# Gather buffers reused as weight buffers, earlier splits of the first tail weights, wider level spacing, one softmax step

## Chip, cores and metric

The kernel runs on one core of a Trainium2 chip. The metric is the device time of one execution in microseconds (us), lower is better. Before the change, three executions took 1249.47, 1243.44 and 1245.83 us, a median of 1245.83 us.

## What is computed

Two blocks in sequence on 256 tokens of width 1024, all float32. The first block ends in PEER: every token picks, in each of 8 heads, 16 of 16384 small experts, and sums their outputs. The second block sends its normalised input through four branches and merges them under gates.

```
act = gelu(einsum('td,thkd->thk', xb, u[expert]))             # 8 heads x 16 experts a token
h   = h + einsum('thk,thkd->td', g * act, v[expert])          # PEER, after a gated-linear-attention mixer
x   = rms_norm(h, norm_f_g)
cols = rms_norm(x, norm_pre) @ w_in_2                          # second block
y_a = deltanet(...); y_b = spatial_gating(gelu(gm_uv), ...)    # gm_uv: the columns called Z_GU, Z_GV here
y_c = sliding_window(softmax with one sink a head); y_m = memory_attention(...)
merged = sum over 4 branches of sigmoid(gate) * (y @ w_up);  out = x + rms_norm(merged @ w_out, norm_post)
```

## The kernel before

**Tiling.** Tokens go in two batches of 128 (b = 0, 1), one token a partition. Weights come as tiles of 128x1024 float32 (512 KB), four to a group, in one fixed order (`STREAM`). Groups named in `SPLIT` are multiplied in two parts: ScalarE (ACT) rounds a tile to `hi` (L207, `cut`), VectorE (DVE) or GpSimd (POOL) subtracts to get `lo` (L208), and TensorE (PE) makes three matmuls of 512 columns (L356 to L358) where a plain float32 product would take one.

**Front and gather stage.** After the first mixer (until about 144 us) the PEER runs in 256 slots, one per batch, head and rank (`peer`). A slot gathers 128 rows of 2048 float32 (1 MB) from `peer_uv` by an indirect DMA that POOL issues (L826) into a buffer `uv`; DVE takes the dot product with the first half of each row (L854); ACT does gelu, weight and diagonal (L858, L859, L865); PE adds the second half into `acc` (L877), or, in some slots, DVE adds it to `x` (L871). A buffer is free after that. Buffers come from `pair`: six of `pairs` at first, then, once the pool `early` of the second batch's mixer is closed (`more_pairs`), four more of `late`. The same pool `pairs` holds split weights (`wp`) in the front and in the tail.

**Order.** All instructions are in an order written out by hand through generators. `gathers` (L892) runs one slot of `peer` after another, and between slots a step of `routes` (expert selection) by a rate per slot and a step of `shadow`: the second batch's mixer, then memory projections, and, for the first batch of the second block, pre-norm, projections, delta net, `sliding(0)` and `memory_attn(0)`. `mixer_levels(1, 3)` takes one level per 3 + 1 steps. In `sliding`, the exponentials (L1355, L1358) are spread over five steps, so that gelus of slots stand between them; ACT loads a function table at each change between them (ACT_TABLE_LOAD).

**End of the gather stage.** `Z_GU`'s four tiles, loaded long before, are split after the last gather's issue (`n <= i < n + 4`, alternately DVE and POOL); `Z_GV`'s four tiles are loaded on ACT's DMA queue in four late sums. `last_out(1)` (L912) adds `acc`, takes two norms and the transposes that feed the second block, with `Z_GV`'s splits between its steps.

**Tail.** The second block's second batch and everything split runs from about 891 us. `wt` keeps `depth` = 4 further tiles loaded and `ahead` = 3 further tiles split, in program order of PE's use; tiles lie in the pool `big` of 28 buffers, in turn with other data. `SyncE` (SP) issues their loads, and a load waits until its buffer's last reader is done. Splits alternate between POOL (even tile) and DVE (odd tile). `pace` mixes branch work between the projections.

```
pair: k = turn["at"] % turn["ring"];  (pairs if k < N_PAIR else late["pairs"]).tile([P, 2048], ...)
AHEAD, LAG = (3, 4), (2, 3)     # slots from gather to dot, from dot to sum; with 6 and with 10 buffers
```

Of the kernel before, what the change touches and what calls it, by code (L numbers as in the profile page):

```python
# [9 lines left out]
F32 = mybir.dt.float32  # L10
# [4 lines left out]
AF = mybir.ActivationFunctionType  # L15
# [4 lines left out]
P = 128  # L20
T = 256
NB = T // P
# [5 lines left out]
N_SLOT, N_PAIR = 28, 6  # L28
# [107 lines left out]
def chain(*gens):  # L136
    for g in gens:
        yield from g
# [3 lines left out]
def kernel(ctx, tc, I, out, dbg=None):  # L142
# [6 lines left out]
    pairs = ctx.enter_context(tc.tile_pool(name="pairs", bufs=N_PAIR))  # L149
    work = ctx.enter_context(tc.tile_pool(name="work", bufs=2))  # L150
    psum = ctx.enter_context(tc.tile_pool(name="psum", bufs=3, space=PSUM))
    first, late = ctx.enter_context(ExitStack()), {}
    early = first.enter_context(tc.tile_pool(name="early", bufs=N_EARLY))
    ctx.enter_context(tc.manual_schedule())

    def slot(name, dt=F32):

        return big.tile([P, 1024], dt, tag="slot", name=name)
# [17 lines left out]
    def more_pairs():  # L176

        first.close()
        late["pairs"] = ctx.enter_context(tc.tile_pool(name="late", bufs=N_LATE))
        turn.update(at=N_PAIR, ring=N_PAIR + N_LATE)  # L180

    def dump(name, ap, view):
        if name in dbg:
# [15 lines left out]
    def load_to(n, queue=nc.sync):  # L199
        while state["next"] < min(n, 4 * G_END):  # L200
            i = state["next"]
            raw[i] = slot(f"w{i}")
            queue.dma_start(out=raw[i], in_=I["wts"][4 * STREAM[i // 4] + i % 4])
            state["next"] += 1

# [4 lines left out]
    def cut_to(n, eng=None):  # L210
        for i in range(state["cut"], min(n, state["next"])):
            if is_split(i):
                if i // 4 in (Z_GV, G_O2 + 1):
                    hi, lo = slot(f"wh{i}", F32R), slot(f"wl{i}", F32R)
                else:
                    wp = pair(f"wp{i}", F32R)
                    hi, lo = wp[:, :1024], wp[:, 1024:]
                cut(raw[i], hi, lo, eng or (G if state["pool"] and i % state["share"] == 0 else V))
                parts[i] = chunks(hi), chunks(lo)
        state["cut"] = max(state["cut"], min(n, state["next"]))  # L220
# [94 lines left out]
    def halves_rstd(x, junk, adds, meanwhile=lambda: None):  # L315

        ss = small("ssh", 2)
        for nh in range(2):
            s = slice(nh * 512, (nh + 1) * 512)
            adds[nh](s)  # L320
            S.activation(junk[:, s], x[:, s], AF.Square, scale=D ** -0.5, accum_out=ss[:, nh:nh + 1])
        r = rstd2(ss)
        meanwhile()
        return r
# [514 lines left out]
    def peer():  # L839


        n = len(all_slots)
        tiles, wv, dg, dve = {}, {}, {}, {}
        dots = diags = sums = 0
        for i in range(n + AHEAD[1] + LAG[1]):
            ahead, lag = AHEAD[state["late"]], LAG[state["late"]]
            state["left"] = n + ahead + lag - i
            if i < n:
                yield from until(routed, all_slots[i][:2])
                tiles[i] = gather(*all_slots[i])  # L850
            while dots < min(n, i - ahead + 1):
                b, h, s = all_slots[dots]
                t = tiles[dots][:, :D]
                V.scalar_tensor_tensor(t, t, 1.0, hn[b], op0=OP.mult, op1=OP.mult,  # L854
                                       accum_out=act[:, h, s:s + 1])
                yield from until(routed, (b, h, "w"))
                ge, wv[dots] = small("ge", 1), small("wv", 1, bufs=6)
                S.activation(ge, act[:, h, s:s + 1], AF.Gelu)  # L858
                S.activation(wv[dots], ge, AF.Copy, scale=gw[b][:, h, s:s + 1])  # L859
                dots += 1  # L860
            while diags < min(dots, i - ahead - lag + 3):
                dve[diags] = on_dve(*all_slots[diags])
                if not dve[diags]:
                    dg[diags] = small("dg", P, bufs=3)
                    S.activation(dg[diags], ident, AF.Copy, scale=wv[diags])  # L865
                diags += 1
            while sums < min(diags, i - ahead - lag + 1):
                b, h, s = x = all_slots[sums]
                t = tiles.pop(sums)[:, D:]
                if dve[sums]:  # L870
                    V.scalar_tensor_tensor(xr[b], t, wv[sums], xr[b], op0=OP.mult, op1=OP.add)  # L871
                else:
                    start = b not in acc
                    if start:
                        acc[b] = psum.tile([P, 2, 512], F32, tag="acc", bufs=1, name=f"acc{b}")
                    for nh in range(2):
                        TE.matmul(acc[b][:, nh], dg[sums], t[:, nh * 512:(nh + 1) * 512],  # L877
                                  start=start, stop=h == 7 and s == 15)
                    pe(1.8)
                if b == NB - 1 and h == 7 and 8 <= s < 12:  # L880
                    load_to(4 * Z_GU + 2 * (s - 7), S)
                if b and h == 0 and s == 1:
                    run(peer_out(b - 1))
                    routed["out", b - 1] = True
                sums += 1
            if n <= i < n + 4:
                cut_to(4 * Z_GU + 1 + i - n, G if i % 2 else V)
            yield

    def gathers(main, routes, rate, others):  # L890
# [25 lines left out]
    def last_out(b):  # L916

        x, junk, a, nf = xr[b], hn[b], acc[b], rowt["nf"]

        def add(s):  # L920
            V.tensor_tensor(out=x[:, s], in0=x[:, s], in1=a.rearrange("p a n -> p (a n)")[:, s], op=OP.add)

        def scale(s):
            V.scalar_tensor_tensor(x[:, s], x[:, s], r, nf[:, s], op0=OP.mult, op1=OP.mult)

        r = halves_rstd(x, junk, (add, add))
        cut_to(4 * Z_GV + 1, G)
        yield
        r2 = halves_rstd(x, junk, (scale, scale), lambda: cut_to(4 * Z_GV + 2, V))
        dump("x2", x, lambda d: d[b * P:(b + 1) * P])  # L930
        dr = small("dg", P, bufs=3)
        V.tensor_scalar(dr, ident, r2, None, op0=OP.mult)
        cut_to(4 * Z_GV + 4, G)
        yield
        hT[b] = slot3(f"hT{b}", 8)
        hh2[b] = slot3(f"hh{b}", 8, P, F32R), slot3(f"hl{b}", 8, P, F32R)

        def put(h, pt):
            s = slice(4 * h, 4 * h + 4)
            gained(hT[b][:, s], pt, chan[:, C_NP:C_NP + 8], h)  # L940
            cut(hT[b][:, s], *[t[:, s] for t in hh2[b]])

        yield from transposed(x, put, scale=dr)
# [386 lines left out]
    def sliding(b):  # L1330
# [21 lines left out]
        V.scalar_tensor_tensor(m, m, sc_, sk, op0=OP.mult, op1=OP.max)  # L1352
        V.tensor_scalar(nm, m, -1.0, None, op0=OP.mult)
        V.tensor_tensor(out=es, in0=sk, in1=m, op=OP.subtract)
        S.activation(es, es, AF.Exp)  # L1355
        yield
        for h in range(8):
            S.activation(sc[:, h], sc[:, h], AF.Exp, scale=sc_, bias=nm[:, h:h + 1], accum_out=su[:, h:h + 1])  # L1358
            if h % 2:
                yield  # L1360
        V.tensor_tensor(out=su, in0=su, in1=es, op=OP.add)
        V.reciprocal(su, su)
# [201 lines left out]

    def shadow():
        yield from rest
        yield from mixer_levels(1, 3)
        yield from mixer_out(1)
        score["mixed"] = True
        yield from peer_norm(1)  # L1570
        for h in range(8):
            yield from until(score, (0, "of", h))
            yield from peer_scores(1, h)
            if h == 4:
                load_memory()
                yield from step(block2_consts)
            if h == 6:
                load_to(4 * G_MEM + 4)
        state["depth"] = 4
        yield from memory()  # L1580
        yield from step(mask_swT)
        yield from until(routed, ("out", 0))
        yield 8.0
        yield from pre2(0)
        yield from small_proj(0)
        yield from qkv(0)
        yield from q_proj(G_SWQ, "swq", 0)
        yield from q_proj(G_XMQ, "xmq", 0)
        state["depth"] = 0
        yield from deltanet(0)  # L1590
        yield from together(sliding(0), memory_attn(0))
        pre2_cut(0)

    state["late"] = 0
    run(gathers(peer(), routes(), lambda i: 0.75 if i < 12 else 0.6 if i < 100 else 0.36, shadow()))
    state["pool"] = True


    rowt["gm"] = slot("row_gm")[:, :512]
    state["share"] = SHARE  # L1600

    state["ahead"] = -1
    lo, sp = last_out(1), chain(spatial_u(Z_GU, "gmu", [0]), spatial_u(Z_GV, "gmv", [0]))
    next(lo)
    for _ in range(4):
        next(sp)
    next(lo)
    for _ in range(2):
        next(sp)
    run(lo, sp)  # L1610
    state.update(depth=4, ahead=3)
    run(spatial_u(Z_GU, "gmu", [1]))
    run(spatial_u(Z_GV, "gmv", [1]))

    def tail_main():
        yield from small_proj(1)
# [116 lines left out]
```

## Time and profile before

| quantity | us |
|---|---|
| median of three executions | 1245.83 |
| the profiled execution, and its span | 1244.99, 1243.2 |
| PE busy | 1065.9 (86%) |
| DVE busy | 873.8 (70%) |
| ACT busy | 514.0 (41%) |
| POOL busy | 457.9 (37%) |
| L877 acc matmuls, 832 | 425.7 |
| L854 dots, 256 | 307.9 |

The page shows the DMA engines' mean share in 40 slices: 9 tenths or more from the 7th slice to the 27th (186 to 839 us), 7 in the 28th (839 to 870 us), and 6 to 0 afterwards. So the stages have different limits, and the rows below are taken by stage. A DMA share slightly over 1 is rounding of overlapping packets. A wait is idle time just before an instruction, with the event that came last.

### The profile page before, as it was taken

Reading aid. Unit: us, or ns where it says so; the run is one execution under the profiler, and the core shown is the slowest. Engines: PE = TensorE matmul, PEld = TensorE weight load, DVE = VectorE, ACT = ScalarE, POOL = GpSimd, SP = SyncE. Lnnn points to the kernel's source line nnn. Section 1 sums busy time; section 2 is a strip of 40 time slices with the busy share of each in tenths; the row PEclk is TensorE's granted clock in tenths of the full one; section 3 lists DMA queues with packets and bytes.
Section 4 is the critical chain, followed back from the end, with each engine's and each line's share of the span. In section 5 each row is a group of like instructions: output and inputs, shape, how many; then the busy total and the mean of one; then the engine's idle time right before and its main releaser. Section 6 shows DMA issues by size and latency. Waiting matters only on the chain.

```text
span 1243.2 us, 14731 instructions
## 1 busy us (share of the span) xinstructions
PE 1065.9 (86%) x4934; PEld 735.1 (59%) x4934; DVE 873.8 (70%) x1823; ACT 514.0 (41%) x1272; POOL 457.9 (37%) x331
## 2 busy tenths in 40 slices
PE   7999879879997969838878888878699899799987
PEld 6876535444565626315445445434389788687876
DVE  5598578896777688788889899754716476248554
ACT  5615233443443434324436444466533433244432
POOL 3314224343534344433433535633310333135531
PEclk9998979989999989969899989998889899899999
DMA  9626489999999999999999999997446433355620
GB/s 367 214 80 216 177 351 356 352 400 426 425 425 425 422 425 426 425 427 384 412 425 424 381 385 422 426 426 299 167 161 237 137 119 119 97 207 183 246 81 34
DMA packets 68074, 376.38 MB, mean 303 GB/s; under 512 B 7696, under 2 KB 8992, under 8 KB 35232
## 3 DMA queue, kind: packets, MB, share of 16 engines
q0 software_dynamic: 36864, 268.45, 52.5%
q1 hardware_dynamic: 28688, 101.47, 22.7%
q10 hardware_dynamic: 2448, 5.54, 1.2%
q8 instruction: 39, 0.64, 0.2%
q14 instruction: 35, 0.29, 0.1%
HBM read 374.38 MB, written 1.05 MB: 302 GB/s over the span
## 4 chain that ended last, share of the span: by engine, by line
PE 33%; DVE 29%; DMA 15%; issue 11%; ACT 7%; POOL 5%; ACTq 0%; POOLq 0%; DVEq 0%; SPq 0%
DMA uv<-in_peer_uv_dram,idx 11%; DVE uv L854 9%; PE acc L877 7%; DVE wp L208 3%; POOL wp L208 2%; DMA w<-in_wts_dram 2%; POOL uv L826 2%; DVE x L871 2%; PE qkv L382 2%; PE pq L382 1%; ACT wp L207 1%; PE mk L382 1%; PE gate L356 1%; PE gate L357 1%; PE gate L358 1%
## 5 line engine op out<-in xcount | busy, mean ns | idle before, releaser
L877 PE MATMUL acc<-uv,dg 128*128 128x512 f32 x832 | 425.7, 648 | 99.6 <-ACT dg L865 88.7
L826 POOL DMA_INDIRECT uv<-in_peer_uv_dram,idx x256 | 304.6, 1190 | 436.4 <-PE acc L877 278.1
L854 DVE SCALAR_TENSOR_TENSOR uv<-uv,hn 128x1024 f32<-128x1024 f32 x256 | 307.9, 1219 | 71.1 <-DMA uv<-in_peer_uv_dram,idx 66.0
L877 PEld LDWEIGHTS acc<-uv,dg 128*128 128x128 f32 x832 | 158.8, 205 | 284.7 <-issue 150.8
L208 POOL TENSOR_TENSOR wp<-w,wp 128x1024 fp32r<-128x1024 f32 x48 | 127.8, 2668 | 276.2 <-ACT wp L207 270.9
L858 ACT ACTIVATE ge<-act 128x1 f32<-128x1 f32 x256 | 51.6, 202 | 351.0 <-DVE uv L854 350.0
L208 DVE TENSOR_TENSOR wp<-w,wp 128x1024 fp32r<-128x1024 f32 x60 | 98.3, 1650 | 94.4 <-ACT wp L207 94.4
L207 ACT CAST wp<-w 128x1024 fp32r<-128x1024 f32 x108 | 108.1, 1047 | 51.5 <-DMA w<-in_wts_dram 36.8
L865 ACT ACTIVATE dg<-mats,wv 128x128 f32<-128x128 f32 x208 | 81.0, 390 | 24.6 <-PE acc L877 23.4
L859 ACT ACTIVATE wv<-ge,gw 128x1 f32<-128x1 f32 x256 | 75.4, 295 | 8.3
L382 PEld LDWEIGHTS pq<-hnT,w 128*128 128x128 f32 x512 | 61.5, 193 | 11.5 <-issue 11.0
L871 DVE SCALAR_TENSOR_TENSOR x<-uv,wv,x 128x1024 f32<-128x1024 f32 x48 | 61.5, 1282 | 4.9 <-ACT wv L859 4.9
L382 PE MATMUL pq<-hnT,w 128*128 128x128 f32 x512 | 62.3, 276 | 0.0
L357 PE MATMUL gate<-wp,hh 128*128 128x512 f32 x128 | 50.1, 392 | 1.9 <-DVE wp L208 1.9
L356 PE MATMUL gate<-wp,hh 128*128 128x512 f32 x128 | 51.7, 404 | 0.0
L358 PE MATMUL gate<-wp,hl 128*128 128x512 f32 x128 | 49.9, 390 | 0.0
L382 PEld LDWEIGHTS qkv<-hT,w 128*128 128x128 f32 x384 | 45.6, 195 | 4.9 <-issue 4.6
L382 PE MATMUL qkv<-hT,w 128*128 128x128 f32 x384 | 45.7, 278 | 0.0
L858 ACT ACT_TABLE_LOAD x24 | 30.8, 1283 | 10.6 <-DMA wsm<-in_w_small_dram 10.2
L1440 ACT ACTIVATE gate<-gate 128x512 f32<-128x512 f32 x16 | 9.6, 598 | 51.9 <-PE gate L358 49.3
L357 PEld LDWEIGHTS gate<-wp,hh 128*128 128x128 f32 x128 | 24.2, 189 | 6.9 <-DVE wp L208 2.4
L358 PEld LDWEIGHTS gate<-wp,hl 128*128 128x128 f32 x128 | 24.2, 189 | 5.2
(500 smaller groups left out, 1832.8 us busy)
## 6 DMA issues: line engine op xcount, KB each, us to landing
w<-in_wts_dram SPq DMA_DIRECT2D x184, 512.0 KB
uv<-in_peer_uv_dram,idx POOLq DMA_INDIRECT x256
w<-in_wts_dram ACTq DMA_DIRECT2D x4, 512.0 KB
wsm<-in_w_small_dram ACTq DMA_DIRECT2D x8, 132.0 KB
x<-in_x_dram SPq DMA_DIRECT2D x2, 512.0 KB
skT<-in_skT_dram ACTq DMA_DIRECT2D x2, 512.0 KB
mem<-in_mem_dram SPq DMA_DIRECT2D x2, 512.0 KB
out_dram<-o SPq DMA_DIRECT2D x4, 256.0 KB
```

Source lines behind the costliest of these rows:

```text
L207: S.copy(hi, x)
L208: (eng or V).tensor_tensor(out=lo, in0=x, in1=hi.bitcast(F32), op=OP.subtract)
L357: TE.matmul(ps, fh, sl, start=False, stop=False)
L358: TE.matmul(ps, fl, sh, start=False, stop=stop)
L382: TE.matmul(ps, wt(g, c)[:, s], x, start=c == 0, stop=c == KC - 1)
L826: G.indirect_dma_start(out=t, out_offset=None, in_=I["peer_uv"], in_offset=bass.IndirectOffsetOnAxis(ap=idx[b][:, h, s:s + 1], axis=0))
L854: V.scalar_tensor_tensor(t, t, 1.0, hn[b], op0=OP.mult, op1=OP.mult, accum_out=act[:, h, s:s + 1])
L858: S.activation(ge, act[:, h, s:s + 1], AF.Gelu)
L859: S.activation(wv[dots], ge, AF.Copy, scale=gw[b][:, h, s:s + 1])
L865: S.activation(dg[diags], ident, AF.Copy, scale=wv[diags])
L871: V.scalar_tensor_tensor(xr[b], t, wv[sums], xr[b], op0=OP.mult, op1=OP.add)
L877: TE.matmul(acc[b][:, nh], dg[sums], t[:, nh * 512:(nh + 1) * 512], start=start, stop=h == 7 and s == 15)
```

## The change

- `more_weights` closes the late gather buffers after the gathers and opens in their memory a pool `tail` of eight 128x1024 buffers for the tail's weights. The ring of `pair` goes back from ten to six. `depth` becomes 7, `ahead` 2 (they were 4 and 3). Six tiles of the next group(s) are asked for at once.
- `Z_GU`'s splits go from the drain into slots n-10, n-8, n-6 and n-4, all on DVE, into buffers of `big` (`Z_GV`'s now go into `pair`). Two of `Z_GV`'s tiles are loaded in these slots, on SP's queue; the other two after `more_weights`. `last_out` no longer has splits between its steps.
- In the tail's start, `Z_GU` of batch 1 comes before `Z_GV` of both batches.
- `mixer_levels(1, 4)`: one more step per level. `routes` goes at 0.58 instead of 0.6 steps per slot up to slot 100.
- `sliding(0)`'s exponentials are one step; `sliding(1)`, in the tail, keeps its steps.

```diff
+    def more_weights():
+        second.close()
+        late["weights"] = ctx.enter_context(tc.tile_pool(name="tail", bufs=2 * N_LATE))
+        turn.update(at=0, ring=N_PAIR)
...
-            raw[i] = slot(f"w{i}")
+            if "weights" in late:
+                raw[i] = late["weights"].tile([P, 1024], F32, tag="tail", name=f"w{i}")
+            else:
+                raw[i] = slot(f"w{i}")
...
-                if i // 4 in (Z_GV, G_O2 + 1):
+                if i // 4 in (Z_GU, G_O2 + 1):
...
-                if b == NB - 1 and h == 7 and 8 <= s < 12:
-                    load_to(4 * Z_GU + 2 * (s - 7), S)
...
-            if n <= i < n + 4:
-                cut_to(4 * Z_GU + 1 + i - n, G if i % 2 else V)
+            if n - 10 <= i < n - 2 and i % 2 == 0:
+                cut_to(4 * Z_GU + 1 + (i - n + 10) // 2, V)
+                load_to(4 * Z_GV + (i - n + 8) // 2)
...
         r = halves_rstd(x, junk, (add, add))
-        cut_to(4 * Z_GV + 1, G)
         yield
-        r2 = halves_rstd(x, junk, (scale, scale), lambda: cut_to(4 * Z_GV + 2, V))
+        r2 = halves_rstd(x, junk, (scale, scale))
...
-        cut_to(4 * Z_GV + 4, G)
...
-        S.activation(es, es, AF.Exp)
-        yield
+        if state["pool"]:
+            S.activation(es, es, AF.Exp)
+        yield
+        if not state["pool"]:
+            S.activation(es, es, AF.Exp)
         for h in range(8):
             S.activation(sc[:, h], sc[:, h], AF.Exp, ...)
-            if h % 2:
+            if h % 2 and state["pool"] or h == 7:
                 yield
...
-        yield from mixer_levels(1, 3)
+        yield from mixer_levels(1, 4)
...
-    run(gathers(peer(), routes(), lambda i: 0.75 if i < 12 else 0.6 if i < 100 else 0.36, shadow()))
+    run(gathers(peer(), routes(), lambda i: 0.75 if i < 12 else 0.58 if i < 100 else 0.36, shadow()))
...
+    more_weights()
     state["ahead"] = -1
-    lo, sp = last_out(1), chain(spatial_u(Z_GU, "gmu", [0]), spatial_u(Z_GV, "gmv", [0]))
+    lo, sp = last_out(1), spatial_u(Z_GU, "gmu", [0])
     next(lo)
...
-    run(lo, sp)
-    state.update(depth=4, ahead=3)
+    run(sp)
+    load_to(4 * Z_GV + 4)
+    run(lo)
+    state.update(depth=2 * N_LATE - 1, ahead=2)
+    load_to(4 * G_AGAIN + 2 * N_LATE - 2)
     run(spatial_u(Z_GU, "gmu", [1]))
-    run(spatial_u(Z_GV, "gmv", [1]))
+    run(spatial_u(Z_GV, "gmv"))
```

**Three places where instructions move.** On ACT, in the first batch's sliding attention (`sws` its scores, `sw_es` the sink, `ge`, `wv`, `dg` of the slots, `msc` the memory attention's scores), before:

```order
L1355 ACT_TABLE_LOAD
L1355 ACTIVATE sw_es<-sw_es 128x8
L858 ACT_TABLE_LOAD
L858 ACTIVATE ge<-act 128x1
L859 ACTIVATE wv<-ge,gw_137 128x1
L865 ACTIVATE dg<-mats,wv 128x128
L1358 ACT_TABLE_LOAD
L1358 ACTIVATE sws,sw_su<-sws,sw_nm 128x128 x2
L1417 COPY msc<-mt 128x512
```

and now:

```order
L867 ACTIVATE ge<-act 128x1
L868 ACTIVATE wv<-ge,gw_137 128x1
L874 ACTIVATE dg<-mats,wv 128x128
L1365 ACT_TABLE_LOAD
L1365 ACTIVATE sw_es<-sw_es 128x8
L1367 ACTIVATE sws,sw_su<-sws,sw_nm 128x128 x8
L1426 COPY msc<-mt 128x512
L867 ACT_TABLE_LOAD
L867 ACTIVATE ge<-act 128x1
```

The eight exponentials and the sink stand behind one table load, with no slot between them; before, each pair had a load ahead of it and one behind it.

On DVE, the last slots of the gather stage and the start of `last_out` (`w` a raw tile, `wp` or `wl` its split, `rst` and `dg` the norm), before:

```order
L854 SCALAR_TENSOR_TENSOR uv,act<-uv,hn_2471 128x1024
L871 SCALAR_TENSOR_TENSOR x_76<-uv,wv,x_76 128x1024
L854 SCALAR_TENSOR_TENSOR uv,act<-uv,hn_2471 128x1024
L208 TENSOR_TENSOR wp_6209<-w_4802,wp_6209 128x1024
L854 SCALAR_TENSOR_TENSOR uv,act<-uv,hn_2471 128x1024
L871 SCALAR_TENSOR_TENSOR x_76<-uv,wv,x_76 128x1024 x2
L921 TENSOR_TENSOR x_76<-x_76,acc_3997 128x512 x2
L311 TENSOR_SCALAR rst_6234<-ssh 128x1
L924 SCALAR_TENSOR_TENSOR x_76<-x_76,rst_6234,row_nf 128x512 x2
L311 TENSOR_SCALAR rst_6272<-ssh 128x1
L208 TENSOR_TENSOR wl_6276<-w_6191,wh_6275 128x1024
L932 TENSOR_SCALAR dg<-mats,rst_6272 128x128
```

and now:

```order
L217 TENSOR_TENSOR wl_6161<-w_4823,wh_6160 128x1024
L863 SCALAR_TENSOR_TENSOR uv,act<-uv,hn_2563 128x1024 x3
L880 SCALAR_TENSOR_TENSOR x_76<-uv,wv,x_76 128x1024
L863 SCALAR_TENSOR_TENSOR uv,act<-uv,hn_2563 128x1024 x2
L880 SCALAR_TENSOR_TENSOR x_76<-uv,wv,x_76 128x1024
L863 SCALAR_TENSOR_TENSOR uv,act<-uv,hn_2563 128x1024 x2
L880 SCALAR_TENSOR_TENSOR x_76<-uv,wv,x_76 128x1024 x2
L929 TENSOR_TENSOR x_76<-x_76,acc_3988 128x512 x2
L320 TENSOR_SCALAR rst_6241<-ssh 128x1
L932 SCALAR_TENSOR_TENSOR x_76<-x_76,rst_6241,row_nf 128x512 x2
L320 TENSOR_SCALAR rst_6269<-ssh 128x1
L939 TENSOR_SCALAR dg<-mats,rst_6269 128x128
```

The last split (`wl_6161`) stands seven dots ahead of the last sum; none is left between the last two dots, nor between the norms and `dg` (L932, now L939).

On ACT, in the tail, where the gate's tanh of one weight group ends (L1440, now L1449) and the casts of the next group follow, before:

```order
L1440 ACTIVATE gate_7666<-gate 128x512
L1440 ACTIVATE gate_7667<-gate 128x512
L207 CAST wp_7870<-w_7818 128x1024
L207 CAST wp_7881<-w_7868 128x1024
L207 CAST yT_7892<-pt 128x512
L207 CAST wp_7918<-w_7879 128x1024
```

and now:

```order
L1449 ACTIVATE gate_7676<-gate 128x512
L1449 ACTIVATE gate_7677<-gate 128x512
L216 CAST wp_7880<-w_7734 128x1024
L216 CAST wp_7891<-w_7792 128x1024
L216 CAST yT_7902<-pt 128x512
L216 CAST wp_7928<-w_7803 128x1024
```

The rows read alike, but the tile behind the two tanhs is another: `wp_7870` is a group's fourth tile, subtracted by DVE; `wp_7880` is its third, subtracted by POOL.

## Rows read from the trace of the kernel before

**Rows 1.** Stretches: length; PE, PEld, DVE, ACT, POOL busy; PEclk; DMA share; GB/s.

```profile
170.00:250.00 80.00, 70.03 (x277) 38.96 (x278) 67.73 (x166) 31.91 (x98) 30.79 (x27) 0.91 0.90 338
250.00:600.00 350.00, 292.91 (x1197) 171.68 (x1196) 276.65 (x682) 128.88 (x418) 144.57 (x124) 0.94 1.01 420
...
800.00:820.00 20.00, 17.70 (x61) 8.86 (x60) 14.09 (x37) 7.58 (x27) 10.33 (x10) 1.00 1.01 426
820.00:840.00 20.00, 11.08 (x27) 4.76 (x26) 10.40 (x20) 16.76 (x37) 5.50 (x5) 0.91 1.01 428
840.00:860.00 20.00, 16.73 (x52) 9.51 (x53) 9.09 (x18) 16.21 (x43) 5.44 (x5) 0.84 0.66 246
...
922.00:1080.00 158.00, 142.27 (x911) 127.79 (x911) 82.20 (x153) 61.83 (x115) 36.61 (x16) 0.95 0.45 149
1080.00:1243.00 163.00, 151.27 (x716) 125.55 (x714) 90.50 (x89) 63.95 (x88) 64.38 (x26) 0.98 0.43 155
```

**Rows 2.** ACT in time, first batch's attention: start, duration, instruction, idle before it.

```profile
825.19 1.28 ACT L858 ACT_TABLE_LOAD   x1
826.48 0.20 ACT L858 ACTIVATE ge<-act 128x1 f32<-128x1 f32 x1
...
832.71 1.28 ACT L1358 ACT_TABLE_LOAD   x1
834.00 0.40 ACT L1358 ACTIVATE sws<-sws,sw_nm 128x128 f32<-128x128 f32 x1
...
834.79 0.56 ACT L1417 COPY msc<-mt 128x512 f32<-128x512 f32 x1
```

**Rows 3.** POOL in time, gathers of that stretch and later splits.

```profile
828.77 0.94 POOL L826 DMA_INDIRECT uv<-in_peer_uv_dram,idx  x1 [5.33 <-DVE sws L1347]
...
844.29 0.94 POOL L826 DMA_INDIRECT uv<-in_peer_uv_dram,idx  x1 [7.80 <-PE acc L877]
...
854.55 1.03 POOL L826 DMA_INDIRECT uv<-in_peer_uv_dram,idx  x1 [7.60 <-PE acc L877]
...
882.25 2.35 POOL L208 TENSOR_TENSOR wp<-w,wp 128x1024 fp32r<-128x1024 f32 x1 [10.49 <-ACT wp L207]
...
893.78 2.92 POOL L208 TENSOR_TENSOR wl<-w,wh 128x1024 fp32r<-128x1024 f32 x1
```

**Rows 4.** DVE in time, the last slots and the norms behind them.

```profile
884.42 1.27 DVE L208 TENSOR_TENSOR wp<-w,wp 128x1024 fp32r<-128x1024 f32 x1 [2.29 <-ACT wp L207]
885.61 1.21 DVE L854 SCALAR_TENSOR_TENSOR uv<-uv,hn 128x1024 f32<-128x1024 f32 x1
...
893.71 3.55 DVE L924 SCALAR_TENSOR_TENSOR x<-x,rst,row_nf 128x512 f32<-128x512 f32 x2 [0.69 <-POOL rst L312]
...
900.18 2.37 DVE L932 TENSOR_SCALAR dg<-mats,rst 128x128 f32<-128x128 f32 x1
```

**Rows 5.** ACT in time, beside those last slots.

```profile
887.30 1.03 ACT L207 CAST wp<-w 128x1024 fp32r<-128x1024 f32 x1
888.24 0.40 ACT L865 ACTIVATE dg<-mats,wv 128x128 f32<-128x128 f32 x1
```

**Rows 6.** What PE waited for in the tail: total, times, longest.

```profile
PE mo L1423 <- ACT msc L1417: 7.6, 1, 7.6
PE pt L335 <- DVE dg L932: 4.5, 1, 4.5
PE prev L1344 <- ACT sws L1346: 2.9, 1, 2.9
PE gate L357 <- DVE wp L208: 1.9, 1, 1.9
```

**Rows 7.** The chain of waits in the tail: start, duration, what.

```profile
1061.01 0.23 PE gate L356
...
1072.95 3.24 DMA w<-in_wts_dram
```

**Rows 8.** ACT in time, end of a gate group in the tail.

```profile
1154.53 0.60 ACT L1440 ACTIVATE gate<-gate 128x512 f32<-128x512 f32 x1 [4.90 <-PE gate L358]
```

## Blind prediction

> **What bounds the kernel now.** I read the busy time by stretches first, because the whole-span shares average over stages with different limits; then, for each stage whose limit the change touches, the instructions in time on the engine that is late, then PE's waits and the chain of waits in the tail.
>
> From 250 to 600 us the DMA engines are full (share 1.01, 420 GB/s) while PE, DVE and ACT all have room [rows 1]. A gather of 128 x 2048 x 4 bytes = 1.05 MB takes 1.05 / 0.426 = 2.46 us at the rate of 800 to 820 us [rows 1], and that is the time of a slot. The change moves no byte out of this stage, so it can only win where the engines are not full. There are three such places. From 170 to 250 us the share is 0.90: 8 us idle, and DVE is busy for 67.73 of 80 [rows 1]. From 840 to 860 us it is 0.66: 6.8 us idle, behind a stretch in which ACT is busy 16.76 and 16.21 of 20 us [rows 1], and POOL stands 5.33, 7.80 and 7.60 us before a gather's issue [rows 3]. Last, the drain: after the last gather has landed nothing but the last dots, sums and norms is on the path.
>
> From 922 us on PE is the bound: 142.27 of 158 and 151.27 of 163 us, with DMA at 0.45 and 0.43 [rows 1]. Its waits there are few and mostly single: 7.6 us for `msc`, 4.5 for `dg`, 2.9 for `sws`, 1.9 for a split weight [rows 6]. The chain shows why two of them exist: `msc` and `sws` are copies queued on ACT behind a cast whose tile has not landed; the chain has a stretch of 3.24 us on a weight's DMA at 1072.95, just before `msc` [rows 7].
>
> **The change, part by part.**
>
> *Mixer levels.* The same DVE work is spread over 7 more slots (7 levels, one step each), through the stretch with the 8 us of idle DMA. If DVE's lumps cause that idle, up to 8 us come back. But the mixer's buffers are also the ones that become the four late gather buffers, so the six-buffer pipeline lasts 7 slots longer, in a stretch where a slot now takes 2.46 / 0.90 = 2.73 us instead of 2.46: 7 x 0.27 = 1.9 us against it, and up to 4 if those slots lag more. I take -2 within (-6, +4). The slower `routes` rate (0.58 for 0.6) is 2 steps in 88 slots, less than one head's selection; nothing for it, since routes run ahead of their slots.
>
> *Exponentials in one step.* Between the copy of the scores and the last exponential there are 12 table loads now and 6 after (the order shows each pair's two loads go). A load is 1.28 us, and the gelu starts 0.01 us after its end (825.19 + 1.28 = 826.47, then 826.48; the same at 832.71 and 834.00 [rows 2]). So ACT loses 6 x 1.28 = 7.7 us of work out of 33 in 40 us. In exchange one stretch of ACT without a slot becomes long: 1.28 + 9 x 0.40 + a copy of 0.56 + 1.28 = 6.7 us [rows 2], that is 2.7 slots. Ten buffers with a lead of 4 slots and a lag of 3 cover 7 slots, so I count it hidden; if the cover is used up, 6.7 - 2.46 = 4.2 us come back. The idle DMA of 6.8 us should fall to about 1.8: -5. Against it stand two of the `Z_GV` tiles that are now loaded between the last gathers: 2 x 0.52 MB / 0.426 = 2.46 us of a full DMA: +2.4. Sum -2.6, within (-7, +2).
>
> The Trainium skill ("ScalarE: Activation LUTs", section "What ACT_TABLE_LOAD costs") states that every switch to another set costs about 2.66 us, a load of 1.28 and a drain of 1.38. By it ACT would lose 16 us, and the whole 6.8 us of idle DMA would go, 1.8 more than I take. The rows agree on the load and contradict the drain: there is 0.01 us behind a load.
>
> *Drain.* Now the last dot (885.61) stands behind a split that waited 2.29 us for its cast on ACT and took 1.27 [rows 4]; without them it starts 3.5 us earlier. Between the last gelu and the last diagonal ACT makes one more cast of 1.03 us [rows 5], of which 0.85 delays the diagonal. -4.4, within (-6, -2). The four splits now stand in the slots n-10 to n-4, on DVE: 4 x 1.27 = 5.1 us of DVE and 4 x 1.03 on ACT, in slots where DVE is busy 14.09 of 20 us and the DMA sets the pace [rows 1]: hidden; without the cover at most 5 us. POOL's queue loses its two splits there (2.35 us [rows 3]), which nobody waits for once DVE makes them.
>
> *`last_out`.* L924's two halves took 3.55 us and `dg` 2.37 [rows 4] while POOL subtracted `wl` beside them (893.78, 2.92 [rows 3]); one split stands between the second norm and `dg`. Without the neighbour I take 1.3 for L924 and 0.5 for `dg`, which with the split (about 1) makes PE's transposes 4.7 earlier. That is the wait of 4.5 on `dg` [rows 6], but a gain only in part: before, six matmuls of `Z_GV` (6 x 0.23 [rows 7] = 1.4 us) filled it, and they now come later, behind splits that are made only after the casts of `hh`. I take -3, within (-5, +2).
>
> So the tail starts 2 + 2.6 + 4.4 + 3 = 12 us earlier.
>
> *Weights in the tail.* Eight buffers that hold nothing else, and 7 tiles of lead for 4, remove the reason for casts that wait for their tile. The waits to win are those behind late casts: `msc` 7.6, `sws` 2.9, the gate's 1.9 [rows 6], 12.4 in all, and about 1 to 2 of PE's lower clock behind them (0.95 granted in 922 to 1080 against 0.98 after it [rows 1]: 158 x 0.03 = 4.7 us at most). I take -14, within (-19, -4): the load still has to wait on SP's single queue for the eighth-last tile's last reader.
>
> The price is `ahead` 2 for 3. At the end of a gate group ACT runs two tanhs that wait for PE, and the next cast is queued behind them. With three tiles of lead PE needs that tile 3 x 6 matmuls x 0.23 = 4.1 us after the group's end; with two, 2.8. The tanh starts some 0.5 behind PE's last matmul (an estimate: two matmuls' time), the cast 0.5 behind that (the tanh's 0.60 overlaps it [rows 8]) and takes 1.03 [rows 5], 2.0 in all; and now POOL subtracts (2.35 [rows 3]) where DVE did (1.27 [rows 4]): 2.0 + 2.35 = 4.4, so PE waits 1.6 at such a boundary, and at DVE's odd tile nothing. I count 5 boundaries in the order where the first cast behind a wait is POOL's with one to two tiles left, at 0.7 to 1.7: +6, within (+2, +26): the upper end is all 14 group ends at 1.9, the wait on a split weight that the trace has once [rows 6]. Net for the tail -8.
>
> **Sum.** -12 - 8 = -20. The profiled execution took 1244.99, 0.84 under the median; from the median 1245.83 - 20 = 1225.8; I say 1225.
>
> **Rivals.**
>
> *Larger gain.* The splits' price is hidden, since the lo part is needed one matmul later than hi and the group boundaries fill with branch work, and the levels win most of their 8 us: -12 - 14 + 1 and 5 more from the levels: 1216. For it: DMA is at 0.45, so a lead of 7 tiles is cheap. Against: the order does put POOL's split behind the tanhs.
>
> *The gap moves.* The gather stage has a fixed amount of bytes; the long ACT stretch empties the ten buffers just as the five short ones did, and the late levels cost what they gain. Then only drain, `last_out` and half of the tail remain: -4.4 - 3 + 2.4 - 4 = -9, 1237. For it: POOL's waits of 7.80 and 7.60 us [rows 3] came after 30 us of such slots, and a slot is still 2.46 us while ACT stands for 6.7.
>
> *Slower.* The split becomes the tail's limit. The ring of 6 pairs with 2 of lead makes every group's first POOL split late: 14 x 1.9 = 26. The weights being early then gains nothing, because casts no longer wait for a tile but for PE to free a pair. With the gather part at its other end (levels +4, exponentials 0, two tiles +2.4, drain -4.4, `last_out` 0): 26 + 2 = +28, 1273; with the gather part as forecast, 26 - 12 = +14, 1260. It decides from about 18 us of such waits, nine boundaries at 1.9. Against it: at present a split's wait of PE is 1.9, once [rows 6].
>
> **Chances.** Forecast 0.60, with its own range 1214 to 1234; larger gain 0.12; gap moved 0.20; slower 0.08. A difference below 0.5% (6.2 us) can't be told from none here, so faster means under 1239.6. The gap-moved case at 1237 falls half under and half over it: faster 0.60 + 0.12 + 0.10 = 0.82, same 0.10, slower 0.08. The range 1209 to 1242 leaves out the slower case, some of the gap-moved case, and the tip of the larger gain.
>
> **What would show it.** In the trace after: 6 table loads in the attention stretch and a DMA share over 0.85 in the 20 us behind it; 170 to 250 us at 0.92 to 0.95; under 1.5 us between the last dots; `dg` about 0.5 us and PE's wait on it under 1; no wait on `msc` over 2; new PE waits on `POOL wp` of 0.7 to 1.7 at gate boundaries, 6 in all. Wrong would be: PE's waits on splits over 15 us, a new hole in the DMA share behind the one-step exponentials, or `msc` still waiting on a weight's DMA.

## The result, and the profile after

The changed kernel took 1227.55 us (median of four executions, 1225.75 to 1231.69), beside 1247.55 of the kernel before on the same chip: ratio 0.9849, 95% interval 0.981 to 0.9887, so 19 us (14 to 24) faster. Run again with the experiments it was at 0.9861 (0.9843 to 0.9878). The profiled execution took 1228.49 with a span of 1226.4; the one before had 1244.99 and 1243.2, so the two traces differ by only 16.8 us: a kernel's executions scatter by some 6 us, and the profiled one of before was among its shorter ones.

First, where the difference arises, from the starts of the same instructions in the two traces. An offset is after less before; the last column is what the stage alone contributes, beside the forecast.

| point | before | after | offset | stage (forecast) |
|---|---|---|---|---|
| first gather's issue | 144.65 | 146.61 | +2.0 | +2.0 (0) |
| first half of the sum `x + acc`, in `last_out` | 890.71 | 884.78 | -5.9 | -7.9 (-9.0) |
| first `swk` matmul, end of the transition | 922.04 | 912.16 | -9.9 | -4.0 (-3) |
| sixth tanh of the gates | 1118.30 | 1094.19 | -24.1 | -14.2 (-14) |
| end | 1243.22 | 1226.41 | -16.8 | +7.3 (+6) |

The tail shows both of its forecast halves: 14.2 us won until the second gate group, 7.3 given back after it. The stage that ends with the sum was forecast as -2 -5 +2.4 -4.4, and its parts came otherwise: 4.4 us were won up to the issue of gather 240 (of 256, counted from 0; 666.6 for 671.0 us from the first gather's issue), 3.8 more up to the last gather's issue (863.58 for 869.78), and from there to the sum, the drain, 0.3 were lost. The stretches of the trace after, with the columns of [rows 1]:

```profile
170.00:250.00 80.00, 70.24 (x264) 38.14 (x265) 65.43 (x161) 32.98 (x101) 30.42 (x28) 0.94 0.94 353
...
820.00:840.00 20.00, 13.22 (x43) 6.43 (x41) 9.20 (x18) 12.14 (x38) 6.66 (x6) 1.00 1.01 428
840.00:860.00 20.00, 16.90 (x65) 10.37 (x66) 11.07 (x20) 14.37 (x37) 4.77 (x4) 0.83 0.86 320
860.00:880.00 20.00, 12.92 (x24) 4.23 (x22) 15.69 (x21) 7.15 (x21) 2.81 (x3) 0.91 0.58 225
```

From 170 to 250 us the DMA share rose from 0.90 to 0.94, and from 840 to 860 us from 0.66 to 0.86 [rows 1]: 2.8 us idle, of which 845 to 850 us has 2.6. The 0.58 behind that is not a new hole but the end of the gathers, as shorter stretches show:

```profile
860.00:865.00 5.00, 3.77 (x9) 1.44 (x8) 2.97 (x4) 1.93 (x5) 2.81 (x3) 1.00 0.96 360
865.00:870.00 5.00, 2.79 (x6) 1.10 (x5) 2.72 (x4) 2.15 (x5) 0.00 (x0) 0.89 1.00 400
870.00:875.00 5.00, 3.32 (x5) 0.82 (x4) 5.00 (x8) 1.78 (x7) 0.00 (x0) 0.77 0.32 136
875.00:880.00 5.00, 3.04 (x7) 0.87 (x5) 5.00 (x7) 1.29 (x5) 0.00 (x0) 1.00 0.01 3
...
845.00:850.00 5.00, 5.00 (x15) 2.84 (x14) 1.14 (x2) 3.73 (x9) 0.94 (x1) 0.66 0.48 146
```

The DMA engines are full until the last gathers land, but then DVE still has 10 us of dots and sums before it without a break (5.00 of 5 us). That DVE would be behind was not forecast. ACT in time through the one-step exponentials:

```profile
835.13 0.39 ACT L874 ACTIVATE dg<-mats,wv 128x128 f32<-128x128 f32 x1
835.53 1.28 ACT L1365 ACT_TABLE_LOAD   x1
836.83 0.21 ACT L1365 ACTIVATE sw_es<-sw_es 128x8 f32<-128x8 f32 x1
836.94 0.38 ACT L1367 ACTIVATE sws<-sws,sw_nm 128x128 f32<-128x128 f32 x1
...
840.02 0.56 ACT L1426 COPY msc<-mt 128x512 f32<-128x512 f32 x1
840.60 1.28 ACT L867 ACT_TABLE_LOAD   x1
841.89 0.20 ACT L867 ACTIVATE ge<-act 128x1 f32<-128x1 f32 x1
```

Between the diagonal of 835.13 and the gelu of 841.89 ACT serves no slot for 6.4 us, close to the forecast's 6.7; of 12 table loads in this attention 6 are left. POOL's longest wait for a buffer in it is still 8 us, but only one wait is over 5 us, where [rows 3] have three (5.33, 7.80 and 7.60):

```profile
837.83 0.94 POOL L835 DMA_INDIRECT uv<-in_peer_uv_dram,idx  x1 [3.49 <-PE acc L886]
846.82 0.94 POOL L835 DMA_INDIRECT uv<-in_peer_uv_dram,idx  x1 [8.06 <-PE acc L886]
850.39 1.65 POOL L835 DMA_INDIRECT uv<-in_peer_uv_dram,idx  x1 [2.63 <-PE acc L886]
```

Now DVE from the last splits to the norms, the answer to [rows 4]:

```profile
862.41 1.22 DVE L863 SCALAR_TENSOR_TENSOR uv<-uv,hn 128x1024 f32<-128x1024 f32 x1
...
865.46 1.23 DVE L217 TENSOR_TENSOR hl<-hT,hh 128x1024 fp32r<-128x1024 f32 x1 [1.82 <-ACT hh L216]
866.60 1.22 DVE L863 SCALAR_TENSOR_TENSOR uv<-uv,hn 128x1024 f32<-128x1024 f32 x1
...
869.65 1.23 DVE L217 TENSOR_TENSOR wl<-w,wh 128x1024 fp32r<-128x1024 f32 x1 [1.82 <-ACT wh L216]
870.79 1.22 DVE L863 SCALAR_TENSOR_TENSOR uv<-uv,hn 128x1024 f32<-128x1024 f32 x1
...
878.91 1.22 DVE L863 SCALAR_TENSOR_TENSOR uv<-uv,hn 128x1024 f32<-128x1024 f32 x1
...
880.05 1.22 DVE L863 SCALAR_TENSOR_TENSOR uv<-uv,hn 128x1024 f32<-128x1024 f32 x1
...
884.78 1.28 DVE L929 TENSOR_TENSOR x<-x,acc 128x512 f32<-128x512 f32 x2 [0.90 <-PE acc L886]
...
887.79 1.41 DVE L932 SCALAR_TENSOR_TENSOR x<-x,rst,row_nf 128x512 f32<-128x512 f32 x2 [0.70 <-POOL rst L321]
...
891.01 0.29 DVE L939 TENSOR_SCALAR dg<-mats,rst 128x128 f32<-128x128 f32 x1 [0.73 <-POOL rst L321]
...
897.86 2.58 DVE L217 TENSOR_TENSOR wp<-w,wp 128x1024 fp32r<-128x1024 f32 x1 [1.21 <-ACT wp L216]
```

No split stands between the last dots now (1.14 us apart), L932 took 1.41 for 3.55 and `dg` 0.29 for 2.37 [rows 4], now that POOL does not subtract beside them. Before, the POOL splits beside `dg` were not the one at 893.78 [rows 3] but the next two:

```profile
900.09 4.70 POOL L208 TENSOR_TENSOR wl<-w,wh 128x1024 fp32r<-128x1024 f32 x2 [1.07 <-ACT wh L207]
```

and now POOL's first split comes behind `dg`, beside the DVE split at 897.86:

```profile
896.96 2.40 POOL L217 TENSOR_TENSOR wp<-w,wp 128x1024 fp32r<-128x1024 f32 x1 [5.99 <-ACT wp L216]
```

But dots ahead of the last ones are 4.2 us apart (862.41, 866.60, 870.79), where a slot's gather takes 2.46, and each split between them waits 1.82 for its cast. And PE's waits in the tail, the answer to [rows 6]:

```profile
PE gate L366 <- DVE wp L217: 3.5, 2, 2.0
PE swt L1380 <- DVE L L1175: 3.0, 1, 3.0
PE gate L366 <- POOL wp L217: 2.5, 3, 1.1
PE pt L344 <- DVE dg L939: 1.2, 1, 1.2
PE o L366 <- POOL wl L217: 1.2, 1, 1.2
PE mt L1424 <- ACT msc L1420: 1.2, 1, 1.2
PE zgm L366 <- POOL wp L217: 1.2, 1, 1.2
PE up L366 <- POOL wp L217: 1.1, 1, 1.1
```

The waits of `mo` on `msc` (7.6) and of `prev` on `sws` (2.9) are gone, and the wait on `dg` fell from 4.5 to 1.2, a little over the forecast's 1. Waits on split tiles (`wp`, `wl`) have come in their place, 12 us in all over eight kinds (2.3 before), the largest of which stand here; 7.8 of the 12 are on POOL's splits, 4.3 on DVE's. Why the first two waits went is seen on ACT, whose casts in the tail waited for a weight's DMA, before

```profile
ACT wp L207 <- DMA w<-in_wts_dram: 36.1, 10, 6.3
```

and after:

```profile
ACT wp L216 <- DMA w<-in_wts_dram: 1.3, 2, 1.0
```

### The profile page after: what moved, and what is told of

Read it like the earlier page. It is cut to its first block, busy times and chain, and to the rows that moved or that the text cites. A ratio compares the mean times of both kernels' runs of the same rounds, so it can differ in the third digit from the quotient of the medians.

```text
span 1226.4 us, 14725 instructions
## 1 busy us (share of the span) xinstructions
PE 1065.2 (87%) x4938; PEld 732.8 (60%) x4938; DVE 889.3 (73%) x1825; ACT 505.0 (41%) x1267; POOL 450.1 (37%) x328
## 3 DMA queue, kind: packets, MB, share of 16 engines
HBM read 374.38 MB, written 1.05 MB: 306 GB/s over the span
## 5 line engine op out<-in xcount | busy, mean ns | idle before, releaser
L217 POOL TENSOR_TENSOR wp<-w,wp 128x1024 fp32r<-128x1024 f32 x48 | 128.6, 2689 | 265.8 <-ACT wp L216 265.2
L217 DVE TENSOR_TENSOR wp<-w,wp 128x1024 fp32r<-128x1024 f32 x60 | 108.9, 1828 | 78.8 <-ACT wp L216 78.8
L1449 ACT ACTIVATE gate<-gate 128x512 f32<-128x512 f32 x16 | 9.6, 598 | 53.6 <-PE gate L367 53.6
L1042 DVE SCALAR_TENSOR_TENSOR qkvT<-qkvr,chan,qkvT 128x128 f32<-128x128 f32 x72 | 24.1, 352 | 5.7 <-ACT qkvT L1040 4.0
```

Of the source, the lines that this page charges most:

```text
L217: (eng or V).tensor_tensor(out=lo, in0=x, in1=hi.bitcast(F32), op=OP.subtract)
```

## Experiments

Times are ratios to the kernel before on the same chip, with 95% intervals; a gain in us beside a ratio is its distance from 1 times 1247. The changed kernel's own ratio is 0.985 to 0.986.

**The changed kernel again** (no edit).

Expected: 

> The changed kernel once more, on the chip of the next three, so that each can be set against it. Expected 0.985 of the kernel before (about 1228 us), and in the trace the same places: the last sum of the gather stage 6 us earlier, the first tail projection (swk) 10 us earlier, the end 17 to 20 us earlier.

Measured: 0.9861 (0.9843 to 0.9878), 1228.56 us; last sum 5.6 us earlier, `swk` 9.5, end 17.1. It serves as the reference for the rest.

**One-step exponentials alone**, in the kernel before.

```diff
-        S.activation(es, es, AF.Exp)
-        yield
+        if state["pool"]:                     # false in the gather stage
+            S.activation(es, es, AF.Exp)
+        yield
+        if not state["pool"]:
+            S.activation(es, es, AF.Exp)
         for h in range(8):
             S.activation(sc[:, h], sc[:, h], AF.Exp, ...)
-            if h % 2:
+            if h % 2 and state["pool"] or h == 7:
                 yield
```

Expected: 

> The kernel before with the one-step exponentials alone. Theory (the ACT time of the table loads starves the gathers): 6 loads of 1.28 us go, the DMA share in the 20 us behind the attention rises from 0.66 to over 0.8, and the time falls by 3 to 5 us (ratio about 0.997). Rival (the gap moves: one long stretch of ACT empties the buffers as five short ones did): DMA share behind it stays under 0.72, and the time stays within 1.5 us.

Measured: 0.9956 (0.9938 to 0.9973), that is -5.5 us (-7.7 to -3.4). In its trace gather 240 is issued 7 us later than in the trace before (the edit acts only after it), so the stretches are set 7 us later:

```profile
827.00:847.00 20.00, 11.38 (x30) 4.77 (x29) 10.98 (x23) 14.36 (x39) 4.83 (x5) 0.82 1.01 426
847.00:867.00 20.00, 19.95 (x77) 11.21 (x76) 10.45 (x17) 10.88 (x34) 8.29 (x7) 0.93 0.90 340
867.00:887.00 20.00, 14.47 (x28) 5.43 (x28) 15.40 (x23) 9.15 (x27) 8.15 (x5) 0.84 0.92 359
```

The share behind the attention is 0.90, so 2.0 us are idle where 6.8 were, and 0.92 after that: the gap did not move. ACT is busy for 14.36 + 10.88 = 25.2 us of the first 40, where it had 33.0 [rows 1]: 7.7 less, the six loads. From gather 240 to the last sum the trace is 6.8 us shorter. The theory holds, with a gain at the upper end of its 3 to 5 us; the rival falls.

**Levels and routes rate alone**, in the kernel before.

```diff
-        yield from mixer_levels(1, 3)
+        yield from mixer_levels(1, 4)
...
-    ... 0.6 if i < 100 ...
+    ... 0.58 if i < 100 ...
```

Expected: 

> The kernel before with levels five slots apart and the routes rate 0.58 alone. Theory as forecast: -2 us (ratio 0.998), with a DMA share of 170 to 250 us up from 0.90 by 0.02 to 0.05 and a later swap to ten buffers. Rival 1: the spread mixer gives back most of the idle 8 us, -5 us or more (0.996). Rival 2: the six-buffer stretch being longer eats it, 0 to +3 us.

Measured: 0.9985 (0.9969 to 1.0002), -1.9 us (-3.9 to +0.2); DMA share from 170 to 250 us 0.93 in its trace. This agrees with the forecast's -2, but its interval reaches zero, so that there is a gain at all in the time of this kernel is likely and not shown. Up to gather 240 the gain does show: from the first gather's issue to that one, the three traces without the wider spacing (before, the exponentials alone, the tail's buffers alone) take 671.0 to 674.6 us and the eleven with it 664.8 to 670.5, with a DMA share from 170 to 250 us of 0.86 to 0.90 and 0.92 to 0.94. In the trace of this run gather 240 comes 6.2 us sooner, but from there to the last sum it takes 78.7 us for 75.1, so that only 2.6 are left: a gain in one stage can be lost again in the next.

**The splits of the last slots taken apart**, in the changed kernel; `cast_one` and `lower_one` are the two halves of `cut`.

```diff
             if n - 10 <= i < n - 2 and i % 2 == 0:
-                cut_to(4 * Z_GU + 1 + (i - n + 10) // 2, V)
+                cast_one(4 * Z_GU + (i - n + 10) // 2)       # ACT: hi
                 load_to(4 * Z_GV + (i - n + 8) // 2)
+            if n - 10 <= i < n - 2 and i % 2:
+                lower_one(4 * Z_GU + (i - n + 10) // 2)      # DVE: lo
```

Expected: 

> The changed kernel with each of the four splits of the last ten slots taken apart: ACT's cast in an even slot, DVE's subtraction one slot (one dot) later. Theory (in the changed kernel DVE waits 1.8 to 2.3 us in front of each subtraction for a cast that itself waits for the dot just before, so a slot takes 4.2 us and not 2.46): the four waits go, the last dot comes 4 to 7 us earlier, and the time is 3 to 6 us under the changed kernel (about 0.981 of before). Rival (DVE's plain work of dots, sums and subtractions, or the landing of the gathers beside the two weight tiles, sets the pace there): the waits go, but the last dot moves by under 1.5 us and the time stays within 1.5 us of the changed kernel.

Measured: 0.9804 (0.9784 to 0.9824), 1221.77 us, 6.8 under the changed kernel. DVE's waits from 845 to 885 us, of the changed kernel:

```profile
DVE wl L217 <- ACT wh L216: 11.2, 4, 5.3
DVE hl L217 <- ACT hh L216: 1.8, 1, 1.8
```

and with the splits apart:

```profile
DVE wl L237 <- ACT wh L233: 5.5, 3, 4.1
...
DVE hl L217 <- ACT hh L216: 0.7, 1, 0.7
```

Its last dot comes at 874.29 (880.05 in the changed kernel), its last sum 11.7 us earlier than in the kernel before (5.9 in the changed kernel). The theory holds. So the four splits were not hidden in their slots: DVE waited for a cast, the cast stood behind the gelu of the dot just done, and the next dot behind the split.

**The tail's buffers alone**, in the kernel before: `more_weights` as in the change.

```diff
     run(lo, sp)
-    state.update(depth=4, ahead=3)
+    more_weights()
+    state.update(depth=2 * N_LATE - 1, ahead=2)
+    load_to(4 * G_AGAIN + 2 * N_LATE - 2)
```

Expected: 

> The kernel before with the tail's buffers alone: eight weight buffers in the late gather buffers' memory, a ring of six pairs, lead 7, splits two tiles ahead; splits in the drain, levels and exponentials as before. Theory: the tail itself shortens by 6 to 8 us from swk to the end (ratio about 0.9945), with 14 us gained up to the middle of the gates and some 7 lost after it to waits on split tiles. Rival: the weights were late because of the load queue's order, and gain under 2 us without the earlier start.

Measured: 0.995 (0.9934 to 0.9965), -6.2 us (-8.2 to -4.4). In its trace 10.5 us are won between the second and the sixth tanh of the gates (45.4 for 55.9 us, where `msc` waited in [rows 6]), 1.2 between `swk` and the second, and some 7 lost after the sixth, as the theory says; the net of 4.4 in this trace is under its 6 to 8. The rival, a gain under 2 us, falls.

**Five buffers and a lead of four**, in the changed kernel.

```diff
-        ... tc.tile_pool(name="tail", bufs=2 * N_LATE) ...
+        ... tc.tile_pool(name="tail", bufs=5) ...
-    state.update(depth=2 * N_LATE - 1, ahead=2)
-    load_to(4 * G_AGAIN + 2 * N_LATE - 2)
+    state.update(depth=4, ahead=2)
+    load_to(4 * G_AGAIN + 3)
```

Expected: 

> The changed kernel with five weight buffers and a lead of four tiles in place of eight and seven (splits two ahead). Theory 1 (what helps is a buffer that nothing else holds): within 2 us of the changed kernel, since PE takes 1.4 us or more per tile and a load some 5. Theory 2 (the length of the lead helps): 4 us or more slower, with ACT's casts waiting for their tiles again, msc among what waits behind them.

Measured: 1.0019 (1.0004 to 1.0035), 1251.0 us: some 20 us slower than the changed kernel, slower even than before. PE waits for weights directly:

```profile
PE swq L391 <- DMA w<-in_wts_dram: 4.1, 3, 1.8
PE xmq L391 <- DMA w<-in_wts_dram: 4.0, 3, 1.8
PE qkv L391 <- DMA w<-in_wts_dram: 3.8, 5, 1.0
```

The changed kernel has none of these waits. The groups `qkv`, `swq`, `xmq` use whole tiles, and all four of a group stay in use until its end, so that with five buffers one tile of the next group can come. The loss lies there: from the first `qkv` matmul to the first `zgm` it takes 69.2 us for 44.8. From the second tanh on the two kernels take the same time (177.6 us), so five buffers win the 10.5 us behind `msc` as eight do. Theory 1 falls for the whole and holds from there on: where a group of four whole tiles is held, a private buffer is not enough. How far the number of buffers and how far the lead decides is not shown, since the run changed both.

**Seven pairs and six weight buffers**, in the changed kernel.

```diff
-        ... tc.tile_pool(name="tail", bufs=2 * N_LATE) ...
-        turn.update(at=0, ring=N_PAIR)
+        ... tc.tile_pool(name="tail", bufs=6) ...
+        late["pairs"] = ctx.enter_context(tc.tile_pool(name="late7", bufs=1))
+        turn.update(at=0, ring=N_PAIR + 1)
...
-    state.update(depth=2 * N_LATE - 1, ahead=2)
-    load_to(4 * G_AGAIN + 2 * N_LATE - 2)
+    state.update(depth=5, ahead=3)
+    load_to(4 * G_AGAIN + 4)
```

Expected: 

> The changed kernel with 8 KB a partition given to the splits: seven pairs and six weight buffers (lead 5), splits three tiles ahead as before the change. Theory (two tiles of lead are too few behind a tanh, forecast +6): PE's waits on wp in the tail, about 9 us in the changed kernel, fall to 3 or less, and the time falls by 4 to 7 us (ratio about 0.981). Rival: POOL's slow subtraction or the shorter load lead takes it back: within 1.5 us of the changed kernel.

Measured: 0.9816 (0.9799 to 0.9834), 5.6 us under the changed kernel run again by the ratios (4 under its first run), in the expected range. The profiled execution, at 1228.47, was one of its longer ones, and in its trace two effects nearly cancel: from the first `qkv` matmul to the first `zgm` it loses 14.7 us (59.5 for 44.8), where PE waits 6.4 us on weights again, and from there to the end it wins 12.1 (253.7 for 265.8).

**POOL on the odd tiles**, in the changed kernel.

```diff
-  eng or (G if state["pool"] and i % state["share"] == 0 else V)
+  eng or (G if state["pool"] and i % state["share"] == state["share"] - 1 else V)
```

Expected: 

> The changed kernel with POOL subtracting the odd tiles and DVE the even ones, so that the first cast behind the tanhs of a gate group goes to DVE (1.25 us) and not to POOL (2.4 us). Theory: the waits on POOL's splits at these boundaries go, 2 to 5 us faster than the changed kernel. Rival: they pass to the next, odd, tile or DVE's own queue is in the way: within 1.5 us.

Measured: 0.9841 (0.9826 to 0.9857), no difference from the changed kernel that the intervals show; the theory's lower end of 2 us is not ruled out by the time. The trace is on the rival's side: the waits pass on (PE waits of 2.6 us on a DVE split and 2.1 on a cast stand in it), and all on split tiles and their casts sum to 11.4 us, where the changed kernel has 12.3. So which engine subtracts the first tile behind a tanh is not the main cost.

**Three tiles split ahead without a shorter load lead**, in the changed kernel: while whole tiles are used, eight buffers; from `Z_GZ` on six, and in the memory of two a seventh pair.

```diff
+    def seventh_pair():
+        third.close()                                  # the pool "two", bufs=2
+        late["pairs"] = ctx.enter_context(tc.tile_pool(name="seventh", bufs=1))
+        turn.update(at=N_PAIR, ring=N_PAIR + 1)
...
+                two = i < 4 * Z_GZ and i % 4 == 3       # else one of six
...
         yield from q_proj(G_XMQ, "xmq", 1)
+        seventh_pair()
+        state.update(depth=7, ahead=3)
         yield from z_silu(Z_GZ, "zgm")
```

Expected: 

> The changed kernel with eight weight buffers while the tail's projections use whole tiles, then (from Z_GZ on) six of them and a seventh pair in the memory of the other two, splits three tiles ahead, lead 7 throughout. Theory (from the run with seven pairs: three tiles of split lead give some 5 to 6 us from the first gate group on, and only the shorter load lead took 9 us away before it): 4 to 6 us faster than the changed kernel (ratio about 0.981 where that one is 0.985). Rival (six weight buffers are too few for the gates as well, or the swap of the pool stalls the loads): within 1.5 us of it.

Measured: 0.9798 (0.9779 to 0.9816), 1220.65 us, 8 under the changed kernel. Its trace runs within 0.1 us of that of the changed kernel from the last gathers until `zgm`, and ends 9.8 earlier. PE's waits on split tiles in its tail, all of them:

```profile
PE gate L374 <- DVE wp L225: 2.3, 1, 2.3
...
PE gm L374 <- POOL wp L225: 1.1, 1, 1.1
PE zgm L374 <- POOL wp L225: 1.1, 1, 1.1
```

4.5 us for 12. The theory holds, the size is above its range. The third tile and the seventh pair that holds it came together and were not measured apart.

**Both gains, and the split of `hh` taken apart too.** The edits are those of the kernel with the splits apart and of the last one together; then also:

```diff
-        cut(hT[b], *hh2[b])
+        S.copy(hh2[b][0], hT[b])
+        yield
+        V.tensor_tensor(out=hh2[b][1], in0=hT[b], in1=hh2[b][0].bitcast(F32), op=OP.subtract)
...
-        pre2_cut(0)
+        yield from pre2_cut(0)
```

Expected: 

> The same with the subtraction of the last ten slots' splits one slot behind the cast as well. Theory: the two gains lie in stages that follow each other and add: 6.5 + 5 us under the changed kernel, about 1216 us, ratio 0.975 to 0.977. Rival: an earlier start of the tail meets weights that are not there yet, and only the larger of the two remains: 0.980.

Measured without the `hh` edit: 0.9721 (0.9695 to 0.9747), 1212.2 us, 17 us under the changed kernel by the ratios: the two gains (7 and 8) add, with a sum above the expected range.

Expected: 

> The same again with the split of the first batch's normalised input (hh, hl), which stands between the same slots, taken apart in the same way. Theory: one more wait of DVE of 0.7 us goes, and nothing is gained beyond 1 us, since in the kernel with the splits apart DVE's own work after 858 us has hardly an idle stretch left. Rival: another 2 us or more.

Measured with it: 0.9703 (0.9687 to 0.9719), 1209.84 us, no difference that the intervals show. This is the fastest of the kernels, 18 to 20 us under the changed kernel and 37 under the one before.

**No weight tile between the last gathers**, in that last kernel.

```diff
-                load_to(4 * Z_GV + (i - n + 8) // 2)
```

Expected: 

> The kernel with splits apart (hh too), seventh pair and three tiles of split lead, but with no Z_GV tile loaded between the last gathers: all four come after them, into the tail's buffers. It measures the forecast's +2.4 us for two tiles (1.05 MB) in a full DMA. Theory: the last gather lands 2 to 2.5 us earlier and the last sum 1 to 2.5 us earlier; Z_GV's later arrival is hidden behind the norms; 1 to 2.5 us under the kernel with the loads between (about 1208 us, ratio 0.969). Rival 1: DVE's dots, sums and splits set the pace there by now, no change. Rival 2: Z_GV then comes late for the tail's start, 1 to 3 us slower.

Measured: 0.9727 (0.9706 to 0.9749), 1214.05 us: no faster (its trace is 5 us later already at gather 240, ahead of anything that the edit touches). From the issue of gather 240 on, its last gather lands some 2 us sooner, its last sum comes 0.8 sooner, and so does the first `swk` matmul, so `Z_GV` does not come late (rival 2). The price in DMA time is there, near the forecast's 2.4, but DVE's dots, sums and splits absorb most of it (rival 1).

## Why the prediction was right, and where its steps were not

*Levels, -2:* -1.9 measured alone, with an interval that touches zero; up to gather 240 they win more, 4.4 us in the trace of the changed kernel. *Exponentials, -5:* -5.5 alone, and the idle DMA left is 2.0 us, 2.8 in the changed kernel (1.8 in the forecast). The table load behaves as the rows before said: 835.53 + 1.28 = 836.81, and the exponential starts at 836.83. The 2.66 us a switch of the Trainium skill ("ScalarE: Activation LUTs", section "What ACT_TABLE_LOAD costs") does not show here either.

*The two `Z_GV` tiles, +2.4:* the gathers do pay about that, the last sum 0.8, in the one trace that measures it. Mis-sized, on the safe side.

*Drain, -4.4, "hidden" in the slots n-10 to n-4:* this step failed, and the sum hides it. From the last gather's issue to the last dot there are 16.5 us now (863.58 to 880.05), 15.8 before (869.78 to 885.61). I had compared busy times, DVE 14.09 of 20 (of 800 to 820 us, some 40 us ahead of these slots), and not what each instruction stands behind. DVE and ACT each work in the order of their instructions here, and where one waits for the other in each slot the slot takes the round trip: dot, gelu, weight, diagonal, cast, split, next dot, 4.2 us. Taking the cast and the subtraction apart gave 6.8 us, more than the 5 that I had named for a lost cover. That the stage as a whole still came within 1.1 us of its forecast is luck: up to the last gather's issue 8.2 us were won in this trace where levels, exponentials and the two tiles were forecast to give 4.6, and behind it 0.3 was lost where 4.4 were to be won.

*`last_out`, -3:* -4.0 in the trace. PE's transposes came 11.3 us earlier against 5.9 of the sum, but 1.4 of that was lost again by `swk`, as forecast: `Z_GV`'s matmuls no longer fill the wait.

The sizes taken without POOL beside them were near: 1.41 for L932 (1.3), 0.29 for `dg` (0.5), whose neighbour before was the split at 900.09, which [rows 3] do not show. L932 before took 3.55. The Trainium skill ("GPSIMD Engine Reference", section "8. Key points") says that POOL shares its SBUF interfaces with DVE and that they contend where DVE reads two SBUF inputs; the rows of L932, which reads two tensors, agree. The change moved this rather than removed it: the splits of `Z_GV` now run beside each other behind the transposes, at 2.58 on DVE where one alone takes 1.23.

*Tail, -14 and +6:* -14.2 and +7.3 in the trace. The first cause is shown: the run with the buffers alone wins 11.7 us of it, and ACT's casts wait 1.3 us for weights where they waited 36.1. Of the second, the size of the term and its cause, two tiles of lead, are shown by the run with three (and the pair that holds the third): 8 us. My finer account of it, a boundary at which POOL's slow subtraction comes first, does not hold up: changing the engine made no difference clear of noise, and 4.3 of the 12 us were on DVE's splits, which I had put at nothing. The slower rival needed 18 us of such waits; there were 12.

The parts measured alone sum to -1.9 - 5.5 - 6.2 = -13.6; the whole is -17 to -19. Each part has an interval of some 2 us to either side. The 4 to 5 us between would be what drain, `last_out`, the two tiles and the new order of `Z_GU` and `Z_GV` gave together, for -5.0 in the forecast (-4.4 - 3 + 2.4), or levels whose gain is not lost again behind them. They were not measured apart; the trace of the changed kernel gives `last_out` -4.0 and the drain +0.3.

## What to carry to other kernels

An operation moved "into the shadow" of a pipelined loop is hidden only if neither of its halves makes an engine wait in the middle of its other work: put a producer's half one iteration before its consumer's. When memory is turned from one ring into another, count what is held at once (here four tiles to a group's end) before dividing it: a prefetch lead and a conversion lead compete for it, and they can be given it at different times. A forecast's total may be right while two of its terms are wrong, so each needs its own experiment.

## What the runs showed beyond that

Five private buffers with a nominal lead of four were 20 us slower than eight with seven: in the three projections that hold four whole tiles, PE waited 12 us for weights and ACT's casts 12.3 of the tail's 16.8 (1.3 in the changed kernel). Removing 1.05 MB from a full DMA at the end of the gather stage moved its last landing by some 2 us and its last sum by 0.8.
